# Reordering three places of a two-layer decoder trunk: block copies and writes with the solve's priority, first transposes inside the last product, outputs turned later

## The chip, the cores and the metric

The kernel runs on one NeuronCore of a Trainium2 chip. The metric is the device time of one execution in microseconds. The core has a matrix engine (TensorE, PE in the profile, with its weight loads shown apart as PEld), three engines for elementwise work (VectorE = DVE, ScalarE = ACT, GpSimd = POOL) and an engine that here only issues transfers (SyncE = SP). Each engine works through its own list of instructions in order and waits on semaphores for the others. The order in each list is fixed when the program is built.

## What is computed

The reference takes x (512 tokens by 2048 channels) through two residual layers:

```python
for i in range(DEPTH):                       # DEPTH = 2
    hn = rms_norm(x, norm_w[i])
    if i % 2 == 0:
        out = diff_attention_mixer(hn, ...)  # 8 heads, value width 256
    else:
        out, v_first = rwkv7_mixer(hn, ...)  # 32 heads of 64 channels
    x = x + out
```

The first mixer projects hn to q, k, v and gate (2048 x 8192), takes for each head the difference of two causal softmaxes, multiplies by v, normalises, multiplies by the gate and projects back (2048 x 2048):

```python
a = p[:, :, 0] - lam * p[:, :, 1]
o = rms_norm(einsum('bhqk,bkhd->bqhd', a, v), subln_w) * (1 - lambda_init)
return (o * silu(gate)) @ w_out
```

The second one projects to r, k, v, g and two low-rank inputs, and runs a recurrence on a 64 x 64 state for each head:

```python
sa = einsum('bhvk,bhk->bhv', S, a_t)
S = S * w_t + sa[..., None] * b_t + v_t[..., None] * k_t
y = einsum('bhvk,bhk->bhv', S, r_t)
```

Then it normalises y per head, adds a bonus term, multiplies by silu(g) and projects back.

## The kernel before

**Precision and splitting.** All large products are made in three matmuls: each operand is split into a high part (rounded to the engine's fast 32-bit type) and a low part, and hi x hi, hi x lo and lo x hi are added (`mm3`, from L112). A weight tile comes by DMA into `wraw`; `split_w` (L88 to L104) makes its high part `wh` on ACT (L102) and its low part `wl` on DVE (L103), 128 x 1024 at a time. So each weight tile costs an ACT cast, a DVE subtraction and then its matmuls. The activations' parts are `hH` and `hL`.

**Order.** A scheduling layer sets each engine's order. It places the instructions by their readiness and their priority. `high_priority(offset=...)` raises the priority of what stands inside it; there are three levels, AHEAD 2000, SCAN 3000 and SOLVE 4000 (L39). `issue_after` binds an instruction to stand behind another one. Small work is woven into long runs of projection matmuls: a `Chain` (from L120) is a generator that is resumed by `tick` (L144) after a number of projection matmuls, the number that it yields.

**First layer.** For each of 8 heads, q, k, v and gate are projected while the attention of the head before runs as such a generator, over four blocks of 128 tokens: `scores` makes the softmax difference `a`, `turn` transposes it (into PSUM tag "pb") and splits it into `at` and `al`, `weigh` multiplies with V, normalises and makes `y` (DVE L390), `turn_y` transposes `y` (PE L395) and copies it to `yT` (ACT L396). In one step of the loop `turn`, `turn_y`, eight matmuls of the projection, `weigh` and `scores` follow each other.

**The end of the first layer.** The output projection's second half is made with seven products instead of eight, in Strassen's way (`seven`, from L489). `prod` multiplies one weight sum, `take` (from L520, SCAN; L523) adds a finished PSUM product to the residual rows `xq`, and `done` writes rows and sums their squares (ACT L727). The last product is z with form "22", whose weights lie in tiles named ropeC, ropeS and T (old tables' space). After `seven` the rows are normalised in two halves of the tokens: sums and rsqrt, and for the first half eight scales (L771) with normal priority. Then `half_h` transposes the scaled rows two channel blocks at a time (PE L805 into `xT`, PSUM tag "pa"), and `make_h` makes `hH` on ACT (L857) and `hL` on DVE (L858). These feed the low-rank projection `lora`, and all later projections of the second layer.

**Second layer.** The 32 heads are worked in 16 pairs. For pair j, k, r, v and (three pairs later) g are projected, each 16 weight tiles of 128 columns. The recurrence is made in blocks of 64 tokens. `gram` makes the products within blocks (`gp`, PE L1065), copies them to `G` (ACT L1072, four copies of 128 x 512), sums squares (`ssl`, ACT L1076), and writes the triangular parts of `G` and `ssl` to the DRAM tile `ltd` with six transfers that ACT issues (L1078 for ssl, L1084 for G). `t_solve` (priority SOLVE) loads `ltd` in another layout into `LT` (POOL L1118), and inverts all triangles by 31 steps of two DVE operations each (L1129, L1131), started by L1120 and L1121 and closed by L1132. The result goes out to `td`, and comes back as `TT` by four transfers. `t_combine` transposes a part of it on DVE (`T`, L1155), multiplies (`px`, PE L1161 and L1171) and copies (`X` L1164, `G` L1167, `TT` L1174, all ACT). `scan_pair` then goes through 8 blocks in order, each with three small matmuls that depend on each other: `sm` L1242, a copy to `rhs` on ACT (L1245), `sm` L1253, a copy to `VS` on ACT (L1255), `sm` L1260, an update of `VS` on DVE (L1264 or, for the first block, L1267). `t_combine` and `scan_pair` of one pair are one `Chain`, woven into the projections of the next pair with 6 projection matmuls between the steps and 8 behind the last of a block while pairs 3 to 14 are projected (fewer in the others).

`gram` of pair j calls the next step of the chain of pair j-1 behind its own matmuls. That step is the one that issues `px`. In pair j, px's operand T therefore has to be there by about the time at which the next `gram` is done.

Of the kernel before, what the change touches and what calls it, by code (L numbers as in the profile page):

```python
# [13 lines left out]
F32 = mybir.dt.float32  # L14
# [9 lines left out]
P = 128  # L24
# [3 lines left out]
NT = T // P  # L28
# [10 lines left out]
AHEAD, SCAN, SOLVE = 2000, 3000, 4000  # L39
# [293 lines left out]
def attention(g, h, qkT, qkL, sq, V, VL, G, gap, rows=None):  # L333
# [56 lines left out]
        nc.vector.scalar_tensor_tensor(b.y[:], o[:, :256], ro[:], G[:, t, :], ALU.mult, ALU.mult)  # L390

    def turn_y(t):
        pt = g.ps.tile([P, 512], F32, name="yt", tag="pa", bufs=2)
        for i in range(2):
            nc.tensor.transpose(pt[:, i * P : (i + 1) * P], blocks[t].y[:, i * P : (i + 1) * P], g.ident[:])  # L395
        nc.scalar.copy(yT[:, :, t * P : (t + 1) * P], pt[:, :256].rearrange("p (c q) -> p c q", c=2))  # L396

    for i in range(NT + 3):
        if 0 < i <= NT:
            turn(i - 1)  # L400
        if i > 2:
            turn_y(i - 3)
        if i == NT + 2:
            break
        yield 8
        if 1 < i < NT + 2:
            weigh(i - 2)
        if i < NT:
            scores(i)
        yield gap - 8  # L410
# [75 lines left out]
                          accum_op=ALU.add)  # L486


def seven(g, w, load, rows, sums, c1, c2, acc, Ts, banks, done):  # L489

# [70 lines left out]
    done("22")  # L563
    take("21", X)
    for i in range(N):
        prod(z, i, "22", Ts[i], i == 0, i == last)
    take("21", z)
    done("21")
# [16 lines left out]
def flat(t):  # L585

    n = "abc"[: len(t.shape) - 1]
    n = " ".join(n)
    return t[:].rearrange(f"p {n} -> p ({n})").rearrange("p (k c) -> p k c", k=KG)


def layer0(g, aps):
# [86 lines left out]
    with ExitStack() as cx:  # L679
# [78 lines left out]
        def banks(i):  # L758
            if i < 2:
# [3 lines left out]
        T2 = g.work.tile([P, KG, 512], F32, name="T2", tag="yTh", bufs=1)  # L763
        load = loader(g, aps["da_w_out"][0], ((g.wraw, "wraw", 3), (g.work, "V", 1), (g.wraw, "wraw", 3),
                                              (g.work, "G", 1), (g.wraw, "wraw", 3)))
        seven(g, aps["da_w_out"][0], load, rows, sums, 1024, 1536, acc, [flat(g.C), flat(g.S), T2], banks, done)

        rs = g.work.tile([P, NT], F32, name="rs1", tag="rs1", bufs=1)
        ss = g.work.tile([P, NT], F32, name="ss1", tag="ss1", bufs=1)
        def scale(cb, t):  # L770
            nc.vector.tensor_scalar(xs[cb][:, t, :], xs[cb][:, t, :], rs[:, t : t + 1], None, ALU.mult)  # L771

        for half in (slice(0, 2), slice(2, 4)):
            with tc.high_priority(offset=SOLVE if half.start else 0):
                nc.vector.reduce_sum(ss[:, half], g.ssx[:, half], AX.X)
                nc.vector.tensor_scalar(ss[:, half], ss[:, half], 1.0 / D, EPS, ALU.mult, ALU.add)
                rsqrt(g, rs[:, half], ss[:, half], 2, "r4")
                if half.start == 0:
                    for cb in range(4):
                        for t in range(2):  # L780
                            scale(cb, t)
# [10 lines left out]
                with tc.high_priority(offset=AHEAD):  # L792
                    make_h(g, ps, KT + k)

        def half_h(k, half, m):

            ps = g.ps.tile([P, 512], F32, name="xT", tag="pa", bufs=2)
            for i in range(2):
                xq, c0 = xs[(k + i) // 4], (k + i) % 4 * P
                for t in range(2):  # L800
                    tt, at = 2 * half + t, (2 * i + t) * P
                    if c0 == 0 and half:
                        scale((k + i) // 4, tt)
                    with tc.issue_after(m.ins) if m else ExitStack():
                        nc.tensor.transpose(ps[:, at : at + P], xq[:, tt, c0 : c0 + P], g.ident[:])  # L805
            for i in range(2):
                with tc.high_priority(offset=AHEAD):
                    make_h(g, ps[:, 256 * i : 256 * i + 256], KT + k + i, k + i, half)

        pts = [g.ps.tile([P, 512], F32, name="lora", tag=tag) for tag in ("pb", "pc")]  # L810
        lora = [(aps["rw_w_in"][0], 4 * D, 2 * RK)]

# [5 lines left out]
            return m  # L818


        m, wts = None, []
        turns = [(k, half) for half in range(2) for k in range(0, KT // 2, 2)]
        for i, (k, half) in enumerate(turns):
            if i == 0:
                half_h(k, half, m)
            if i + 1 < len(turns):
                half_h(*turns[i + 1], m)
            else:
                more_h(KT // 2 + 1, m)
            if half == 0 and k % 4 == 0:  # L830
                wts.append(split_w(g, lora, 4, 2 * RK, k))
            for kk in (k, k + 1):
                m = products(kk, wts[kk // 4], slice(256 * half, 256 * half + 256), m)
# [68 lines left out]
C = 64  # L902
# [151 lines left out]
def gram(g, j, p, before):  # L1054
# [12 lines left out]
    if before:  # L1067
        with g.tc.issue_after(m.ins):
            before.step(g)
    for c0, gp in halves:  # L1070
        for h in range(2):
            nc.scalar.copy(p.G[:, c0 : c0 + 4, :, h, :], gp[h][:].rearrange("p (u x t) -> p u x t", u=4, x=2))  # L1072
    ps = g.ps.tile([P, 512], F32, name="pt", tag="pb", bufs=2)
    sum_channels(g, ps[:2, :], g.ones[:, 0 : P : C], p.k2)
    ss = w.tile([2, T], F32, name="ssl", tag="thg", bufs=1)
    nc.scalar.copy(ss[:], ps[:2, :])  # L1076
    for half in range(2):
        nc.scalar.dma_start(  # L1078
            out=g.ltd[j % 2, half, :, :, HALF, :],
            in_=ss[:].rearrange("h (c b t) -> h c b t", c=NC_, b=2)[:, :, half, :])  # L1080
    for half in range(2):
        for h in range(2):
            q0 = h * C + half * HALF
            nc.scalar.dma_start(  # L1084
                out=g.ltd[j % 2, half, h, :, 0:HALF].rearrange("c s t -> s c t"),
                in_=p.G[q0 : q0 + HALF, :, 0, h, half * HALF : (half + 1) * HALF])


def mask_gram(g, p, h):
# [421 lines left out]
```

## Time and profile before

| what | us |
|---|---|
| median of three runs | 2210.98 |
| lowest and highest run | 2207.24, 2213.17 |
| the profiled execution | 2206.95 |
| its span in the profile | 2205.2 |
| PE busy | 2171.5 (98%) |
| DVE busy | 1445.4 (66%) |
| ACT busy | 1041.9 (47%) |
| POOL busy | 293.8 (13%) |

The mean granted clock of TensorE over the execution was 0.993 of full speed. Times in the rows of the profile are microseconds from the start of the span. A row of the timeline gives the start, the duration, the engine, the source line, the operation, the output and inputs with their sizes, how many like it were taken together, and in brackets the idle time before it and what ended it. A row of waits gives the waiting engine and tile, what it waited for, the total, the number of waits and the longest. A row of windows gives a stretch of time, its length, the busy time of PE, PEld, DVE, ACT and POOL with their counts of instructions, the granted clock (1.00 is full speed), the busy share of the DMA engines and their rate. ACTq and POOLq are the DMA issues on these engines. Line numbers are those of the kernel before.

### The profile page before, as it was taken

What the parts mean: (1) busy time and instruction counts of PE and PEld (TensorE: products, weight loads), DVE (VectorE), ACT (ScalarE), POOL (GpSimd) and SP (SyncE); (2) the same over time, 40 slices, a digit from 0 to 9 for tenths busy, and PEclk for the clock granted to TensorE, in tenths of its full rate; (3) what the DMA queues carried; (4) which work ended last, traced back from release to release, by engine and by line L of the source; (5) the groups of instructions that cost most, each with busy time, mean ns of one, the idle gap of its engine ahead of it and who ended that gap; (6) DMA issues with size and microseconds to landing.
All of it is one profiled execution on the core that took longest, in us unless ns stands there. A gap on an engine that the chain in (4) does not pass through costs nothing.

```text
span 2205.2 us, 34098 instructions
## 1 busy us (share of the span) xinstructions
PE 2171.5 (98%) x12260; PEld 1767.9 (80%) x12260; DVE 1445.4 (66%) x3780; ACT 1041.9 (47%) x2118; POOL 293.8 (13%) x637
## 2 busy tenths in 40 slices
PE   9999999999999999999999999999999999999999
PEld 7888888888888888878777787878887788877887
DVE  5664646455654666475667877777778877767644
ACT  5443434334443454345455555555555556545322
POOL 0000000000000000110222222222222222221001
PEclk9999999999999999999999999999999999999999
DMA  6223222222323356653422333333333333446555
GB/s 192 96 79 98 84 96 96 86 96 87 96 77 99 131 171 225 158 117 90 106 57 76 81 87 86 93 97 92 91 87 85 96 91 77 113 123 187 172 167 119
DMA packets 296313, 240.20 MB, mean 109 GB/s; under 512 B 47792, under 2 KB 255680, under 8 KB 296144
## 3 DMA queue, kind: packets, MB, share of 16 engines
q1 hardware_dynamic: 256912, 190.13, 29.3%
q0 software_dynamic: 12384, 29.72, 6.3%
q10 hardware_dynamic: 26848, 18.18, 2.7%
q8 instruction: 96, 1.57, 0.3%
q14 instruction: 73, 0.60, 0.1%
HBM read 217.98 MB, written 19.99 MB: 108 GB/s over the span
## 4 chain that ended last, share of the span: by engine, by line
PE 70%; DVE 19%; issue 4%; DMA 3%; ACT 2%; SPq 0%; POOL 0%; ACTq 0%; DVEq 0%; POOLq 0%
PE pp L114 52%; PE pt L114 5%; DVE wl L103 3%; DVE tmpl L1129 3%; DVE Tm L1131 2%; DMA td<-Tm 2%; DVE VS L1264 1%; PE gp L1065 1%; PE sm L1242 1%; PE lora L114 1%; PE sc L114 1%; PE sm L1260 1%; DMA TT<-td 1%; ACT wh L102 1%; PE sm L1253 1%
## 5 line engine op out<-in xcount | busy, mean ns | idle before, releaser
L103 DVE TENSOR_TENSOR wl<-wraw,wh 128x1024 fp32r<-128x1024 f32 (+2 forms) x319 | 388.9, 1219 | 431.5 <-ACT wh L102 419.0
L102 ACT CAST wh<-wraw 128x1024 fp32r<-128x1024 f32 (+2 forms) x319 | 333.5, 1046 | 513.0 <-PE pp L114 378.3
L114 PE MATMUL pp<-wh,hH 128*128 128x512 f32 x1268 | 499.3, 394 | 0.3 <-DVE gs L326 0.2
L114 PE MATMUL pp<-wh,hL 128*128 128x512 f32 x1268 | 497.7, 393 | 0.1
L114 PE MATMUL pp<-wl,hH 128*128 128x512 f32 x1268 | 497.4, 392 | 0.0
L114 PE MATMUL pp<-hH,wl 128*128 128x512 f32 x1024 | 416.1, 406 | 0.3 <-DVE wl L103 0.3
L114 PE MATMUL pp<-hL,wh 128*128 128x512 f32 x1024 | 415.9, 406 | 0.0
L114 PE MATMUL pp<-hH,wh 128*128 128x512 f32 x1024 | 413.1, 403 | 0.0
L114 PEld LDWEIGHTS pp<-wh,hH 128*128 128x128 f32 x1268 | 238.3, 188 | 48.4 <-PE pp L114 0.6
L114 PEld LDWEIGHTS pp<-wh,hL 128*128 128x128 f32 x1268 | 238.3, 188 | 48.4 <-DVE hL L858 0.5
L114 PEld LDWEIGHTS pp<-wl,hH 128*128 128x128 f32 x1268 | 238.4, 188 | 46.4
L114 PEld LDWEIGHTS pp<-hH,wh 128*128 128x128 f32 x1024 | 194.6, 190 | 36.1 <-issue 0.9
L114 PEld LDWEIGHTS pp<-hL,wh 128*128 128x128 f32 x1024 | 194.6, 190 | 34.9
L114 PEld LDWEIGHTS pp<-hH,wl 128*128 128x128 f32 x1024 | 194.7, 190 | 32.9 <-DVE wl L103 0.7
L1129 DVE SCALAR_TENSOR_TENSOR tmpl<-LT,Tm 128x60 f32<-128x60 f32 (+24 forms) x496 | 135.1, 272 | 10.9
L1248 POOL COPY SA<-VS 64x64 f32<-64x64 f32 x224 | 60.9, 272 | 457.0 <-DVE VS L1264 350.0
L459 POOL DMA_DIRECT2D frow<-yd x12 | 8.9, 746 | 796.4 <-DVE rs_i L63 676.8
L1131 DVE TENSOR_TENSOR Tm<-Tm,tmpl 128x60 f32<-128x60 f32 (+24 forms) x496 | 104.0, 210 | 11.2
L1255 ACT COPY VS<-sm 64x64 f32<-64x64 f32 x256 | 52.9, 207 | 65.8 <-PE sm L1253 61.1
L1245 ACT COPY rhs<-sm 64x64 f32<-64x64 f32 x256 | 52.7, 206 | 53.7 <-PE sm L1242 51.3
L1264 DVE SCALAR_TENSOR_TENSOR VS<-sm,gam,Sg 64x64 f32<-64x64 f32 x192 | 54.1, 282 | 24.7 <-PE sm L1260 20.6
L1251 POOL TENSOR_SCALAR Sg<-SA,gam 128x64 f32<-128x64 f32 x96 | 63.3, 660 | 9.5 <-POOL SA L1248 0.2
(333 smaller groups left out, 3189.6 us busy)
## 6 DMA issues: line engine op xcount, KB each, us to landing
wraw<-in_rw_w_in_dram SPq DMA_DIRECT2D x128, 512.0 KB
wraw<-in_da_w_in_dram SPq DMA_DIRECT2D x254, 256.0 KB
wraw<-in_da_w_out_dram SPq DMA_DIRECT2D x26, 512.0 KB
wraw<-in_rw_w_out_dram SPq DMA_DIRECT2D x26, 512.0 KB
LT<-ltd POOLq DMA_DIRECT2D x64, 132.0 KB, 2.9
yr<-yd SPq DMA_DIRECT2D x28, 256.0 KB
frow<-yd POOLq DMA_DIRECT2D x12, 512.0 KB, 6.9
xq<-in_x_dram SPq DMA_DIRECT2D x16, 256.0 KB
```

What stands on the lines that cost most here:

```text
L102: nc.scalar.copy(hi[:, ks], raw[:, ks])
L103: nc.vector.tensor_sub(lo[:, ks], raw[:, ks], hi[:, ks].bitcast(F32))
L114: m = nc.tensor.matmul(out, a, b, start=s, stop=e, skip_group_check=skip)
L1065: m = nc.tensor.matmul(gp[h][:, i * P : (i + 1) * P], BK[r_, c0 + i, :, :], p.AR[r_, c0 + i, :, :], start=True, stop=True)
L1129: nc.vector.scalar_tensor_tensor(tt, LT[:, i : i + 1, i + 1 :].to_broadcast([P, s, n]), n2[:, i : i + 1], Tm[:, 0:s, i : i + 1].to_broadca ...
L1131: nc.vector.tensor_add(Tm[:, 0:s, i + 1 :], Tm[:, 0:s, i + 1 :], tt)
L1242: nc.tensor.matmul(sm[:, 0:P], both(p.G[:, c, 0]), both(VS[:, c]), start=True, stop=True)
L1245: nc.scalar.copy(rhs[r_, :], sm[r_, h * C : h * C + C])
L1248: nc.gpsimd.tensor_copy(p.SA[r_, c - 1, :], VS[r_, c, h, :])
L1251: nc.gpsimd.tensor_scalar(Sg[:], p.SA[:, c - 1, :], p.gam[:, c : c + 1], None, ALU.mult)
L1255: nc.scalar.copy(VS[r_, c, h, :], sm[r_, P : P + C])
L1264: g.state = nc.vector.scalar_tensor_tensor(VS[r_, c + 1, h, :], s_, p.gam[r_, c : c + 1], Sg[r_, :], ALU.mult, ALU.add)
```

## The change

Three places are reordered. The instructions are the same in number and shape in both kernels.

A. `attention`: `turn_y` stands after the eight matmuls and after `weigh`, and its PSUM tile is of tag "pb", of which there is one buffer and which `turn` uses as well. The last `turn_y` of a head keeps its place.

B. The end of the first layer: `seven` gets a function `begin` that it calls ahead of the last product's last weight tile. `begin` normalises the first half of the tokens, now with priority SCAN, and issues the first two `half_h` transposes (into PSUM tag "pp"). The second half is normalised after `seven`, as before, and the lora loop no longer begins with a transpose of its own.

C. `gram`: the four copies to `G`, the copy to `ssl` and the six writes to `ltd` get the priority SOLVE, and the four writes of G are put ahead of the two writes of ssl.

```diff
     def turn_y(t):
-        pt = g.ps.tile([P, 512], F32, name="yt", tag="pa", bufs=2)
+        pt = g.ps.tile([P, 512], F32, name="yt", tag="pb")
...
     for i in range(NT + 3):
         if 0 < i <= NT:
             turn(i - 1)
+        if i == NT + 2:
+            turn_y(i - 3)
+            break
+        yield 8
+        if i > 1:
+            weigh(i - 2)
         if i > 2:
             turn_y(i - 3)
-        if i == NT + 2:
-            break
-        yield 8
-        if 1 < i < NT + 2:
-            weigh(i - 2)
         if i < NT:
             scores(i)
...
-def seven(g, w, load, rows, sums, c1, c2, acc, Ts, banks, done):
+def seven(g, w, load, rows, sums, c1, c2, acc, Ts, banks, done, begin=None):
...
     for i in range(N):
+        if i == last and begin:
+            begin(g.m)
         prod(z, i, "22", Ts[i], i == 0, i == last)
...
-        seven(g, aps["da_w_out"][0], load, rows, sums, 1024, 1536, acc, [flat(g.C), flat(g.S), T2], banks, done)
...
-        for half in (slice(0, 2), slice(2, 4)):
-            with tc.high_priority(offset=SOLVE if half.start else 0):
+        def normalise(half):
+            with tc.high_priority(offset=SOLVE if half.start else SCAN):
                 nc.vector.reduce_sum(ss[:, half], g.ssx[:, half], AX.X)
...
-        def half_h(k, half, m):
-
-            ps = g.ps.tile([P, 512], F32, name="xT", tag="pa", bufs=2)
+        def half_h(k, half, m, bank=(g.ps, "pa", 2)):
+
+            ps = bank[0].tile([P, 512], F32, name="xT", tag=bank[1], bufs=bank[2])
...
+        def begin(m):
+
+            normalise(slice(0, 2))
+            for k in (0, 2):
+                half_h(k, 0, m, (g.pp, "pp", 4))
+
+        seven(g, aps["da_w_out"][0], load, rows, sums, 1024, 1536, acc, [flat(g.C), flat(g.S), T2], banks, done, begin)
+        normalise(slice(2, 4))
...
-        m, wts = None, []
+        m, wts = g.m, []
...
-            if i == 0:
-                half_h(k, half, m)
-            if i + 1 < len(turns):
+            if 0 < i < len(turns) - 1:
                 half_h(*turns[i + 1], m)
-            else:
+            elif i:
                 more_h(KT // 2 + 1, m)
...
-    for c0, gp in halves:
-        for h in range(2):
-            nc.scalar.copy(p.G[:, c0 : c0 + 4, :, h, :], gp[h][:].rearrange("p (u x t) -> p u x t", u=4, x=2))
+    with g.tc.high_priority(offset=SOLVE):
+        for c0, gp in halves:
+            for h in range(2):
+                nc.scalar.copy(p.G[:, c0 : c0 + 4, :, h, :], gp[h][:].rearrange("p (u x t) -> p u x t", u=4, x=2))
...
-    nc.scalar.copy(ss[:], ps[:2, :])
-    for half in range(2):
-        nc.scalar.dma_start(
-            out=g.ltd[j % 2, half, :, :, HALF, :],
-            in_=ss[:].rearrange("h (c b t) -> h c b t", c=NC_, b=2)[:, :, half, :])
-    for half in range(2):
-        for h in range(2):
-            q0 = h * C + half * HALF
+    with g.tc.high_priority(offset=SOLVE):
+        nc.scalar.copy(ss[:], ps[:2, :])
+    with g.tc.high_priority(offset=SOLVE):
+        for half in range(2):
+            for h in range(2):
+                q0 = h * C + half * HALF
+                nc.scalar.dma_start(
+                    out=g.ltd[j % 2, half, h, :, 0:HALF].rearrange("c s t -> s c t"),
+                    in_=p.G[q0 : q0 + HALF, :, 0, h, half * HALF : (half + 1) * HALF])
+        for half in range(2):
             nc.scalar.dma_start(
-                out=g.ltd[j % 2, half, h, :, 0:HALF].rearrange("c s t -> s c t"),
-                in_=p.G[q0 : q0 + HALF, :, 0, h, half * HALF : (half + 1) * HALF])
+                out=g.ltd[j % 2, half, :, :, HALF, :],
+                in_=ss[:].rearrange("h (c b t) -> h c b t", c=NC_, b=2)[:, :, half, :])
```

## The prediction

> **What bounds the kernel now.** I read the page first (busy shares), then the granted clock in narrow windows, then the groups of waits on PE, and last the timeline at the three places that the change touches.
>
> ```profile
> span 2205.2 us, 34098 instructions
> PE 2171.5 (98%) x12260; PEld 1767.9 (80%) x12260; DVE 1445.4 (66%) x3780; ACT 1041.9 (47%) x2118; POOL 293.8 (13%) x637
> ```
>
> TensorE is busy 98% of the span, so everything the change can win is in the 2% of gaps and in time at a lower clock; any work it moves costs nothing until PE waits for it. The windows show where the clock is lost (columns: window, its length, busy times, then PEclk, DMA share, GB/s):
>
> ```profile
> 1090.00:1095.00 5.00, 2.10 (x24) 1.47 (x22) 1.70 (x3) 0.32 (x1) 2.52 (x9) 1.00 0.80 175
> 1095.00:1100.00 5.00, 5.00 (x31) 3.26 (x30) 0.87 (x2) 1.97 (x4) 2.02 (x3) 0.62 0.76 195
> 1100.00:1105.00 5.00, 5.00 (x42) 4.26 (x41) 0.51 (x1) 1.77 (x3) 0.00 (x0) 0.50 0.00 0
> ...
> 1151.00:1161.00 10.00, 10.00 (x69) 7.44 (x67) 1.97 (x2) 4.11 (x9) 0.00 (x0) 0.50 0.33 86
> 1215.50:1219.00 3.50, 3.50 (x25) 2.56 (x23) 3.16 (x13) 1.08 (x2) 0.00 (x0) 0.52 0.61 166
> ...
> 1949.50:1956.50 7.00, 7.00 (x62) 5.87 (x61) 0.00 (x0) 4.17 (x9) 1.78 (x2) 0.51 0.18 46
> ```
>
> ```profile
> PE px L1161 <- DVE T L1155: 12.5, 13, 3.1
> PE yt L395 <- DVE y L390: 1.5, 8, 0.3
> PEld yt L395 <- DVE y L390: 3.9, 7, 0.6
> PEld sm L1260 <- ACT VS L1255: 16.8, 43, 0.8
> PEld sm L1253 <- ACT rhs L1245: 12.4, 33, 0.6
> ```
>
> ```profile
> 1094.37 0.69 PE L1161 MATMUL px<-T,G 32*32 32x32 f32 x16 [2.90 <-DVE T L1155]
> 1148.83 0.69 PE L1161 MATMUL px<-T,G 32*32 32x32 f32 x16 [1.83 <-DVE T L1155]
> 1213.61 0.69 PE L1161 MATMUL px<-T,G 32*32 32x32 f32 x16 [3.06 <-DVE T L1155]
> 1946.32 0.69 PE L1161 MATMUL px<-T,G 32*32 32x32 f32 x16 [0.46 <-DVE T L1155]
> ```
>
> The waits (total us, times, longest) are those of PE and of its weight load (PEld). The largest one that stops PE is px on T, the end of the solve: 7.8 of its 12.5 us in pairs 0 to 2 (2.90, 1.83, 3.06). Behind each of those the clock stands near 0.5, for about 10, 10 and 3.5 us, and for 7 us after the small one of pair 14 at 1946: some 30 us at half, so 15 us lost, more than the waits themselves. That is the prize of part C.
>
> [...]
>
> **Part A, outputs turned 8 matmuls later (first layer).** The same two transposes and one copy per block, in another bank, behind the 8 matmuls and weigh. Eight 128x512 matmuls (one every 0.23 us in the timeline) are 1.8 us, over the longest wait of 0.6. So up to 1.5 + 3.9 = 5.4 us go; part of the weight loads' 3.9 is already under a running matmul, and the last block of each head keeps its place. I take half, **-2.8 us**, bounds -5.4 and 0. The bank is now shared with turn, whose copies end before weigh starts, so no wait comes in its place; what hides it is those same matmuls.
>
> **Part B, first transposes within the last product.**
>
> ```profile
> 969.31 0.48 DVE L771 TENSOR_SCALAR xq<-xq,rs 128x512 f32<-128x512 f32 x1
> 969.71 1.22 DVE L103 TENSOR_TENSOR wl<-ropeC,wh 128x1024 fp32r<-128x1024 f32 x1
> 970.84 2.47 DVE L523 TENSOR_TENSOR xq<-xq,pp 128x512 f32<-128x512 f32 x4
> ```
>
> ```profile
> 971.15 0.39 PE L114 MATMUL z<-wl,hH 128*128 128x512 f32 x1
> 974.50 0.50 PE L114 MATMUL z<-wl,hH 128*128 128x512 f32 x1 [0.24 <-DVE wl L103]
> 980.00 1.25 PE L805 MATMUL xT<-ident,xq 128*128 128x128 f32 x8 [0.18 <-DVE xq L523]
> 982.34 0.47 PE L114 MATMUL lora<-hH,wh 128*96 128x256 f32 x2 [1.08 <-ACT hH L857]
> 982.97 0.36 PE L114 MATMUL lora<-hL,wh 128*96 128x256 f32 x1 [0.15 <-DVE hL L858]
> 984.22 0.36 PE L114 MATMUL lora<-hL,wh 128*96 128x256 f32 x1 [0.27 <-DVE hL L858]
> ```
>
> The transposes and hH/hL now run under the last product, so the listed waits go: 0.24 + 0.18 + 1.08 + 0.15 + 0.27 = 1.9 us. But the eight scales (L771) and the takes (L523) now carry the scan's priority, and in the changed program's order of DVE all of them stand ahead of the split wl of ropeC, which today runs at 969.71, before the takes. The takes can't start before 970.8 (they wait for the last X matmul), take 2.47, two scales behind them 2 x 0.45, the split 1.22: it ends at about 975.4. The second matmul of z needs it at 971.15. New stall about 4.3 us, at one place; net +2.4. A gap of that length stands beside rows where 1.83 to 3.06 us cost 3.5 to 10 us at half clock, which is 1.7 to 5 us; I take 2.5. **+4.9 us**; bounds -1.9 (the split isn't late) and +7.5. [...]
>
> **Part C, block copies and writes with the solve's priority.** Pair 7, a steady one, today:
>
> ```profile
> 1456.05 2.06 ACT L1072 COPY G<-gp 128x512 f32<-128x512 f32 x4
> 1457.97 0.74 ACT L1174 COPY TT<-px 32x256 f32<-32x256 f32 x2
> 1458.50 0.31 ACTq L1084 DMA_DIRECT2D ltd<-G  x1
> 1458.73 0.58 ACT L1076 COPY ssl<-pt 2x512 f32<-2x512 f32 x1
> 1459.37 1.05 ACT L102 CAST wh<-wraw 128x1024 fp32r<-128x1024 f32 x1
> 1460.32 0.20 ACT L1245 COPY rhs<-sm 64x64 f32<-64x64 f32 x1
> ...
> 1463.96 0.31 ACTq L1084 DMA_DIRECT2D ltd<-G  x1
> ```
>
> ```profile
> 1474.86 1.23 DVE L103 TENSOR_TENSOR wl<-wraw,wh 128x1024 fp32r<-128x1024 f32 x1
> 1476.00 0.59 DVE L1264 SCALAR_TENSOR_TENSOR VS<-sm,gam,Sg 64x64 f32<-64x64 f32 x2
> 1476.63 0.18 DVE L1120 TENSOR_SCALAR LT<-LT 128x32 f32<-128x32 f32 x1
> ```
>
> ```profile
> 1057.74 1.23 DVE L103 TENSOR_TENSOR wl<-wraw,wh 128x1024 fp32r<-128x1024 f32 x1 [4.79 <-ACT wh L102]
> 1058.88 0.17 DVE L1120 TENSOR_SCALAR LT<-LT 128x32 f32<-128x32 f32 x1
> ```
>
> On ACT the changed order is: four G copies, first G write, ssl copy, three G writes, two ssl writes, and only then the TT copies (L1174), rhs and wh. So the last write comes about 3 us earlier than 1463.96, the load of LT with it, and the solve's first operation (L1120) stands ahead of the split and the VS update that precede it today: 1.23 + 0.59 and a part of what is before them, some 2 us. T then comes some 2 us earlier in pairs 3 to 15, against waits under 1 us there: px's remaining 12.5 - 7.8 = 4.7 us go, and with them the half clock at 1949.5 (7.0 us, worth 3.4): **-8.1 us**; bounds -8.1 and 0.
>
> In exchange, what stands behind the copies and writes on ACT is late: TT copies and rhs by about 2 us, and with them the scan's first steps of each pair. In the changed order of PE these steps are put later and then closer together: steps of L1260 that stand only 1 or 2 projection matmuls behind the L1253 they depend on go from 11 to 32, steps of L1253 only 2 or 3 behind L1242 from 15 to 23. A short step of this kind costs today 16.8/43 = 0.39 us and 12.4/33 = 0.38 us (weight-load waits). 21 x 0.39 + 8 x 0.38 = 11.2, and 0.8 for the steps of L1242 that move to 4 or 5 matmuls behind L1260 (21 more): **+12 us**, that is 1.1 in each of the 11 steady pairs. Lower bound half of it (+6: weight loads run beside matmuls); upper bound 11 x 2.6 = 29, if each pair's six squeezed steps, rhs behind a split's cast of 1.05 us among them, all show in full (6 x 0.38 is 2.3, and 0.3 more for the cast).
>
> Pairs 0 to 2: the order puts px earlier too, by 6, 3 and 17 projection matmuls, 1.4, 0.7 and 3.9 us at 0.23. In pair 0 the solve starts right behind the split of 1057.74, which waited 4.79 us for ACT's wh; it starts with no wait of its own, so LT was already there, and an earlier LT gains little: 0.5 us. For pairs 1 and 2 I take 1 and 3.5 us, from what the writes and the splits ahead of the solve free (pair 2's writes are spread widest). Waits: 2.9 + 0.9, 1.8 - 0.3, 3.1 + 0.4: **+1.0 us**, and the 23.5 us at half clock behind them stay. Bounds: +6 if T comes no earlier; -7.8 - 11.7 = -19.5 if all three waits and their clock go. I take the value near the upper end since px and T move together.
>
> SP's queue keeps its order; POOL's queue, which issues the loads of LT, only has them earlier.
>
> **Sum.** -2.8 + 4.9 - 8.1 + 12.0 + 1.0 = **+7.0 us** on the profiled execution (2206.95): 2213.95. That execution lies 4.0 below the median of the three runs shown (2210.98); on the median it gives **2218.0**, 0.3% slower; 0.3% (6.6 us) is about what a measurement of this kernel can tell from no change.
>
> **Rivals.**
> 1. *T really comes early (faster).* The copies and writes end the wait that pairs 0 to 2 show, px no longer stands still, and the half clock behind it goes. T must come 4.3, 2.5 and 7.0 us earlier (today's wait and what px was moved); under that it changes nothing. For it: the clock rows, the largest single loss in the trace. Against it: the row of 1058.88, where LT isn't what the solve waits for. It gives 7.0 - 1.0 - 19.5 = -13.5: 2197.
> 2. *Everything hides (no change that shows).* The squeezed steps cost their lower bound, 6, since their weight loads run beside matmuls, and B's stall costs no clock: -2.8 + 2.4 - 8.1 + 6 + 1 = -1.5: 2209.5. For it: PE is busy 98%. That C doesn't bring T earlier at all, so that the -8.1 stays out, ends here too with the low price (+6.6: 2217.6), at the edge.
> 3. *New stalls lower the clock in the steady pairs (clearly slower).* The row of 1946.32 shows 7 us at half clock after a wait of only 0.46 us and a second small one; the squeezed steps put 1 us and more of waits into a few us in each of 11 pairs. One such window of 3.5 us at half costs 1.7: +19, so 2237; two in each pair give 2256. [...]
>
> **Numbers.** Forecast 0.36, rival 1 0.24, rival 2 0.24, rival 3 0.16. Faster 0.27: rival 1 and a tenth of the forecast. Slower 0.46: rival 3 and most of the forecast. Same 0.27: rival 2 and the rest. Forecast's own range 2211 to 2231 (hop cost 6 to 24). The whole range 2194 to 2243 leaves out the deep end of rival 3 and B's and C's lower bounds taken together.
>
> **What would show it.** A: no wait of yt on y but the last of each head. B: a wait of about 4 us of z on wl at the change of layer, no wait of lora on hH, clock near 0.5 behind it. C: ssl writes behind the G writes, L1120 some 2 us earlier in steady pairs, no px wait from pair 3 on, and PEld waits of L1260 and L1253 about 1.1 us larger per pair; px waits of 2 to 4 us in pairs 0 to 2 with half clock behind. Wrong it would be if px shows no wait in pairs 0 to 2, if the split of ropeC ends in time, or if a steady pair's scan waits add nothing.

## The result: slower by 1.0%

The changed kernel takes 2231.39 us (median of 6 runs, 2224.55 to 2237.05); the kernel before takes 2208.64 us (median of 6, 2202.67 to 2213.17). The ratio is 1.0103 with a 95% interval of 1.0079 to 1.0128, so +22.7 us. The forecast was 2218.0 (+7.0 us), in a range of 2194 to 2243.

The profiled execution of the changed kernel was one of its longer ones: 2237.05 us, span 2235.3 us, 30.1 us more than the profiled execution before. In the changed kernel the lines stand 8 to 11 lower: px is L1172, T L1166, the scan's steps L1253, L1264 and L1271 (before: L1242, L1253 and L1260). In the kernels with C alone and its variants they stand 3 lower (px L1164, T L1158, the scan's steps L1245, L1256 and L1263). The page of the changed kernel:

```profile
span 2235.3 us, 34039 instructions
PE 2193.8 (98%) x12260; PEld 1768.8 (79%) x12260; DVE 1433.8 (64%) x3780; ACT 1040.9 (47%) x2118; POOL 311.8 (14%) x637
```

The waits of PE, and of DVE on the transfer of TT, changed kernel:

```profile
DVE T L1166 <- DMA TT<-td: 40.1, 18, 6.0
PEld sm L1271 <- ACT VS L1266: 30.9, 65, 1.0
...
PEld sm L1264 <- ACT rhs L1256: 16.6, 52, 0.6
...
PE px L1172 <- DVE T L1166: 13.7, 14, 3.7
...
PE sm L1271 <- ACT VS L1266: 4.1, 14, 0.8
PE z L114 <- DVE wl L103: 3.8, 1, 3.8
...
PE yt L395 <- DVE y L390: 0.2, 1, 0.2
```

DVE's wait for that transfer in the kernel before:

```profile
DVE T L1155 <- DMA TT<-td: 20.5, 15, 4.5
```

Five things are to be seen against the rows of before. The waits of yt on y are gone (1.5 to 0.2). A single new wait of 3.8 us stands at z, the place that the prediction named. The scan's short steps wait longer: for VS twice as long (30.9 us in the weight loads and 4.1 on PE, in place of 16.8 and 0.8), for rhs a third longer (16.6 in place of 12.4). px waits for T as it did: 13.7 us in place of 12.5; T was not made earlier for px. And DVE itself stands twice as long for TT, 40.1 us in place of 20.5.

The windows at half clock of the changed kernel (the number behind the busy times of the five engines is PEclk, as before):

```profile
974.70:978.10 3.40, 3.40 (x10) 2.66 (x9) 0.22 (x1) 0.31 (x1) 2.38 (x5) 0.50 0.01 2
1097.60:1111.20 13.60, 13.54 (x86) 10.40 (x87) 4.59 (x6) 2.69 (x6) 3.37 (x4) 0.50 0.55 120
1155.60:1165.80 10.20, 10.20 (x68) 7.67 (x67) 1.28 (x2) 4.83 (x10) 1.98 (x4) 0.50 0.36 93
1213.60:1230.70 17.10, 15.99 (x96) 12.29 (x97) 4.83 (x9) 8.37 (x19) 5.05 (x8) 0.50 0.16 41
1343.40:1346.80 3.40, 3.40 (x44) 3.18 (x43) 0.13 (x1) 2.49 (x6) 0.00 (x0) 0.50 0.16 48
```

That is 47.7 us at half, against 30.7 before (10.2, 10.2, 3.4 and 6.8 us); at half speed 8.5 us more are lost. Where the 30.1 us between the two profiled executions lie can be read from where landmarks stand: the z product begins 1.5 us earlier (969.42 for 970.92); the end of the low-rank products is 2.8 us later (1015.9 for 1013.1), so 4.3 were lost between; `gram` of pair 4 is 9.8 later (1278.5 for 1268.7), 7.0 more, all of it longer half clock; `gram` of pair 14 is 33.1 later (1918.8 for 1885.7), 23.3 more in ten steady pairs; and the end is 30.1 later, 3.0 won back, since there is no half clock at pair 14.

### The profile page after: what moved, and what is told of

The parts are those of the page before. It is cut to its first block, busy times and chain, and to the rows that moved or that the text cites. A ratio compares the mean times of both kernels' runs of the same rounds, so it can differ in the third digit from the quotient of the medians.

```text
span 2235.3 us, 34039 instructions
## 1 busy us (share of the span) xinstructions
PE 2193.8 (98%) x12260; PEld 1768.8 (79%) x12260; DVE 1433.8 (64%) x3780; ACT 1040.9 (47%) x2118; POOL 311.8 (14%) x637
## 4 chain that ended last, share of the span: by engine, by line
PE 71%; DVE 17%; ACT 5%; DMA 3%; issue 3%; POOL 0%; SPq 0%; ACTq 0%; DVEq 0%; POOLq 0%
PE pp L114 53%; PE pt L114 5%; DVE tmpl L1140 3%; DVE wl L103 3%; DVE Tm L1142 2%; DMA td<-Tm 2%; ACT wh L102 2%; PE sc L114 1%; DVE VS L1275 1%; PE gp L1073 1%; PE o L114 1%; PE sm L1271 1%; PE z L114 1%; PE sm L1253 1%; DMA TT<-td 1%
## 5 line engine op out<-in xcount | busy, mean ns | idle before, releaser
L114 PE MATMUL pp<-hH,wl 128*128 128x512 f32 x1024 | 421.8, 412 | 0.1
L1259 POOL COPY SA<-VS 64x64 f32<-64x64 f32 x224 | 69.5, 310 | 454.1 <-DVE VS L1275 387.8
L1278 DVE TENSOR_SCALAR VS<-sm,gam 64x64 f32<-64x64 f32 x32 | 9.1, 283 | 124.7 <-PE sm L1271 124.2
L1256 ACT COPY rhs<-sm 64x64 f32<-64x64 f32 x256 | 52.9, 207 | 46.2 <-PE sm L1253 43.4
L1262 POOL TENSOR_SCALAR Sg<-SA,gam 128x64 f32<-128x64 f32 x96 | 72.4, 754 | 9.4
```

Of the source, the lines that this page charges most:

```text
L114: m = nc.tensor.matmul(out, a, b, start=s, stop=e, skip_group_check=skip)
L1256: nc.scalar.copy(rhs[r_, :], sm[r_, h * C : h * C + C])
L1259: nc.gpsimd.tensor_copy(p.SA[r_, c - 1, :], VS[r_, c, h, :])
L1262: nc.gpsimd.tensor_scalar(Sg[:], p.SA[:, c - 1, :], p.gam[:, c : c + 1], None, ALU.mult)
```

## The experiments

How the table is read: every run has its mean granted clock c. Time x (1 - c) is about what the half clock cost in that run (for the profiled execution before: 2206.95 x 0.007 = 15.4, and half of its 30.7 us at half clock is 15.4). The rest, time x c, is the time outside this loss. Differences of means over the runs, each to the kernel before on the same chip in the same series:

| kernel | ratio of times, 95% interval | difference, us | in half clock | outside it |
|---|---|---|---|---|
| changed kernel (A, B and C) | 1.0103, 1.0079 to 1.0128 | +22.2 | +3.9 | +18.2 |
| A alone | 0.9971, 0.9952 to 0.9989 | -5.8 | -3.1 | -2.7 |
| A alone, again | 0.9963, 0.9947 to 0.9979 | -7.2 | -4.3 | -3.0 |
| B alone | 1.0016, 0.9999 to 1.0033 | +3.1 | +0.7 | +2.4 |
| C alone | 1.0082, 1.0054 to 1.0110 | +17.4 | -1.9 | +19.3 |
| B, normal priority | 1.0009, 0.9991 to 1.0026 | +1.2 | +1.8 | -0.6 |
| C, order of writes alone | 1.0031, 1.0013 to 1.0049 | +6.3 | +3.0 | +3.3 |
| C, writes without priority | 1.0034, 1.0014 to 1.0054 | +7.0 | +3.4 | +3.6 |
| C, ssl and writes with AHEAD | 1.0106, 1.0085 to 1.0127 | +20.5 | +9.9 | +10.6 |
| C, writes issued by SP | 1.0077, 1.0056 to 1.0097 | +16.9 | +11.7 | +5.2 |
| C, writes issued by POOL | 1.0041, 1.0024 to 1.0058 | +9.2 | +12.9 | -3.7 |
| C, scan's copies first | 1.0073, 1.0043 to 1.0102 | +16.4 | +8.1 | +8.4 |
| A and B with normal priority | 0.9986, 0.9963 to 1.0010 | -3.9 | +0.8 | -4.7 |

(For the changed kernel, before is 54 runs of it in three other series, for which the clock is on record.) The clock of a run is given to 0.001, which is 2.2 us; means over 4 to 26 runs are better than that. Over 54 runs of the kernel before, the standard deviation was 1.5 us for the time outside the half clock and 4.3 us for the time lost in it. So differences of 2 us and more in the last column mean something, while in the column before it only the large ones do.

### The three parts alone

A alone is the diff's first piece, B alone the pieces of `seven` and of the end of the first layer, C alone the piece of `gram`.

> Only part A (outputs turned 8 matmuls later). My theory: the waits of yt on y go and z begins 1.5 us earlier, as in the changed kernel; nothing else moves: -1.5 to -2 us. Rival (the freed bank order costs as much in turn or scores): 0 or above.

> Only part B. My theory: z waits about 4 us for the split wl of ropeC, one window of 3.4 us at half clock follows, the lora waits go: the end of lora +4 to +5 us against before, and the whole about +4. Rival (the stall in the changed kernel comes from A's shift or is made good later by more cover in pair 0): 0.

> Only part C. My theory (squeezed scan steps): the way from gram of pair 4 to gram of pair 14 is 640 us instead of 617, and the whole is +20 to +27 us, nearly all that the changed kernel lost. Rival (clock): the steady pairs keep about 62 us each and the loss is in the stretches at half clock of pairs 0 to 3, +7 to +10 us in all.

Outside the half clock the parts add up: -2.7 + 2.4 + 19.3 = 19.0, and all three together cost 18.2. The loss is C's. A alone wins more than the 1.5 to 2 us that I expected: its z begins 2.8 us earlier than in the kernel before (968.08 for 970.92), not 1.5. B alone has the same single wait as the changed kernel, 3.80 us of z on wl, at 975.17. Its low-rank products end at 1018.0, 5.0 us later than before, with 6.8 us at half clock behind the wait. On the whole B costs 3.1 us, and its interval touches no change.

C alone needs 637.6 us from `gram` of pair 4 to that of pair 14 where the kernel before needs 617.0. Only 3.4 us of that stretch are at half clock, so the rival that put the loss into the clock of pairs 0 to 3 falls: C alone has less half clock in all than before (13.7 us in its profile). The waits of C alone:

```profile
PEld sm L1263 <- ACT VS L1258: 30.7, 66, 0.7
PEld sm L1256 <- ACT rhs L1248: 16.9, 52, 0.6
...
PE px L1164 <- DVE T L1158: 11.2, 11, 3.7
```

They are those of the changed kernel. To see where the time goes, I take for each matmul at full clock its lateness: by how much it starts later behind its predecessor than the shortest spacing of two such matmuls in the kernel before. Summed over the ten steady pairs, it rose ahead of `sm` L1260 from 3.1 to 14.4 us (1.1 us for each pair; the expectations further down say 15), ahead of L1253 from 1.1 to 3.7, ahead of L1242 from 5.6 to 7.4, and ahead of the projection's matmuls by 4.8. Together that is 20.5 us; the ten pairs cost 18.9 outside the half clock, as a little came back at `gp` (1.1).

### B with normal priority for the first half

```diff
-            with tc.high_priority(offset=SOLVE if half.start else SCAN):
+            with tc.high_priority(offset=SOLVE if half.start else 0):
```

> Part B, but the first half is normalised and scaled with normal priority as before, so that the split of ropeC can run ahead of the scales. My theory: the 4 us wait of z and the half clock behind it go, some of lora's waits stay away: -2 to 0 us against before. Rival (the split is late because the takes are ahead of it, not the scales): as part B alone, +4.

The wait is gone. DVE of this kernel:

```profile
968.59 1.28 DVE L772 TENSOR_SCALAR xq<-xq,rs 128x512 f32<-128x512 f32 x3
969.78 1.22 DVE L103 TENSOR_TENSOR wl<-ropeC,wh 128x1024 fp32r<-128x1024 f32 x1
970.91 2.48 DVE L523 TENSOR_TENSOR xq<-xq,pp 128x512 f32<-128x512 f32 x4
```

The split of ropeC runs ahead of the takes again. In the changed kernel six scales ran first, and the split was late:

```profile
967.00 2.47 DVE L773 TENSOR_SCALAR xq<-xq,rs 128x512 f32<-128x512 f32 x6
969.38 2.47 DVE L524 TENSOR_TENSOR xq<-xq,pp 128x512 f32<-128x512 f32 x4
971.77 0.87 DVE L773 TENSOR_SCALAR xq<-xq,rs 128x512 f32<-128x512 f32 x2
972.57 1.22 DVE L103 TENSOR_TENSOR wl<-ropeC,wh 128x1024 fp32r<-128x1024 f32 x1
```

So it is the priority of the first half's normalisation, not the moved transposes, that makes B cost anything: 2.9 us lie between the two kernels outside the half clock. The moved transposes themselves win 0.6 us outside the half clock, less than these runs can tell from nothing; the 2 us that I had hoped for at best did not come, and the whole is 1.2 us above before.

### C: which of its pieces

The order of the writes alone, with no priority raised:

```diff
-    with g.tc.high_priority(offset=SOLVE):
+    with g.tc.high_priority(offset=0):
         for c0, gp in halves:
...
-    with g.tc.high_priority(offset=SOLVE):
+    with g.tc.high_priority(offset=0):
         nc.scalar.copy(ss[:], ps[:2, :])
-    with g.tc.high_priority(offset=SOLVE):
+    with g.tc.high_priority(offset=0):
         for half in range(2):
             for h in range(2):
```

> Of part C only the order of the writes (G ahead of ssl), without any priority. My theory: the TT copies and rhs stay ahead of the later writes on ACT, so the scan isn't squeezed: gram 4 to gram 14 617 to 620 us, whole -3 to +3. Rival (the order of the writes itself delays LT, since ssl comes last): +5 or more.

The priority on the copies to G and ssl, not on the writes:

```diff
     with g.tc.high_priority(offset=SOLVE):
         nc.scalar.copy(ss[:], ps[:2, :])
-    with g.tc.high_priority(offset=SOLVE):
+    with g.tc.high_priority(offset=0):
         for half in range(2):
             for h in range(2):
```

> Part C with the priority on the copies to G and ssl alone; the writes in the new order with normal priority. My theory: the block of writes is no longer ahead of TT copies and rhs, only the copies are, which they nearly are in the kernel before too (only ssl passes TT, 0.6 us): gram 4 to 14 about 620 us, whole 0 to +5. Rival (the copies' place, not the writes', squeezes the scan): 635 to 640, +20.

Both are slower than before by 0.3%, half of it outside the half clock (+3.3 and +3.6 us). From `gram` of pair 4 to that of pair 14 they need 623.0 and 619.7 us (633.2 less half of 20.5 at half clock, and 619.7 with none; before 617.0). So the new order of the writes costs some 3 us by itself, which I had expected to be nothing; the priority of the copies to G and ssl adds nothing to it that shows. In both, the lateness ahead of L1260 is 8.4 us (3.1 before) and ahead of L1242 9.8 (5.6 before): the scan's steps move already with the order. What remains of C's 19.3, some 16 us, comes with the priority of the writes.

The priority of ssl and the writes lowered from SOLVE to AHEAD, below the scan's:

```diff
-    with g.tc.high_priority(offset=SOLVE):
+    with g.tc.high_priority(offset=AHEAD):
         nc.scalar.copy(ss[:], ps[:2, :])
-    with g.tc.high_priority(offset=SOLVE):
+    with g.tc.high_priority(offset=AHEAD):
         for half in range(2):
```

> Part C with copies to G at the solve's priority, ssl and the writes at the lowest of the three raised priorities (below the scan's). My theory: the scan's copies stand ahead of the writes again, the writes ahead of casts and other work: gram 4 to 14 617 to 622 us, whole -4 to +4. Rival (any earlier write pulls the solve over the splits and squeezes the scan): as part C alone, +20 and more.

My expectation failed: +20.5 us, as much as C alone, though it is made up in another way, 10.6 outside and 9.9 in the half clock. The scan's steps came back in part: the lateness ahead of L1260 is 9.1 us in the ten pairs instead of 14.4 (before 3.1), ahead of L1253 none. But a wait that is small before (1.8 and 1.3 us, two times each) stands at `gram` now. The waits of this kernel:

```profile
PEld gp L1065 <- DVE AR L1049: 7.6, 11, 1.5
...
PE gp L1065 <- DVE AR L1049: 5.8, 9, 1.1
```

### C with the writes taken off ACT

If the scan is late because ACT is busy with the writes, another engine should issue them.

```diff
-                nc.scalar.dma_start(
+                nc.sync.dma_start(
                     out=g.ltd[j % 2, half, h, :, 0:HALF].rearrange("c s t -> s c t"),
...
-            nc.scalar.dma_start(
+            nc.sync.dma_start(
                 out=g.ltd[j % 2, half, :, :, HALF, :],
```

> Part C, with the six writes issued by SP instead of ACT. My theory (the writes hold up ACT, and the scan's copies TT, rhs and VS are late behind them): the scan keeps its 6 and 8 matmuls, the L1260 waits fall from 15 to 3 to 8 us in the ten steady pairs, and gram 4 to 14 takes 615 to 622 us; whole -5 to +5 us. Rival (the solve that begins earlier takes over the splits and updates and that costs the time, whoever issues): 630 us or more, +10 and more. Where px still waits for T, the early solve wasn't worth anything either way.

The same with `nc.gpsimd.dma_start`:

> Part C, with the six writes issued by POOL instead of ACT. My theory: as with SP for ACT's copies, but POOL also makes SA and Sg for the scan, so that its issues (about 1 us each) hold those up: gram 4 to 14 between 620 and 632 us. Rival (early solve): 630 or more, and the same as with SP.

Half of what I expected came. With SP, the lateness ahead of L1260 fell from 14.4 to 3.7 us, as forecast, and that ahead of L1253 to 1.1, the value of before. So the hold-up on ACT was real. But the ten pairs took 651.1 us, of which 40.6 at half clock: 630.8 with the half clock counted out, not 615 to 622 (POOL: 645.3, 37.5 and 626.5). With SP those are the rival's figures (630 or more, +10 and more); its cause, a price of the early solve whoever issues the writes, fits them. The lateness had moved, to L1242 (15.2 us, before 5.6; PE waits there 8.8 us for DVE's update of VS in the whole kernel, before 3.0) and to `gram`. The timelines of PE and DVE of the kernel with SP, at pair 7's end:

```profile
1522.83 0.69 PE L1164 MATMUL px<-T,G 32*32 32x32 f32 x16 [0.89 <-DVE T L1158]
1524.34 3.62 PE L1065 MATMUL gp<-AR,BK 64*128 64x128 f32 x32 [0.82 <-DVE AR L1049]
```

```profile
1520.76 0.44 DVE L1158 STREAM_TRANSPOSE T<-TT 64x256 f32<-64x256 f32 x1 [5.26 <-DMA TT<-td]
1521.13 1.18 DVE L103 TENSOR_TENSOR wl<-wraw,wh 128x1024 fp32r<-128x1024 f32 x1
1522.33 0.44 DVE L1158 STREAM_TRANSPOSE T<-TT 64x256 f32<-64x256 f32 x1
1522.81 0.75 DVE L898 SCALAR_TENSOR_TENSOR mixr<-pp,prmin_rw_mu_dram,mixr 128x511 f32<-128x511 f32 x1
1523.59 0.69 DVE L1049 TENSOR_TENSOR AR<-mixr,E 128x512 f32<-128x512 f32 x1
```

DVE has the two transposes of T ahead of mixr and AR, the first also ahead of the split; in the kernel before, mixr stands ahead of the first and AR ahead of the second. I take it that the scheduler counts on an early T; the traces show only the order. On the chip T isn't early: DVE stands 5.26 us for the transfer of TT with that work behind it. AR is late for `gram`: PE waits 0.82 us there from pair 4 to pair 14, and 0 to 0.89 us at px just ahead of it. At `gram` of pairs 4 to 13 the clock falls to half each time (the 32 matmuls of `gp` above take 3.62 us instead of 2.06). In this profile the steady pairs alone lose 20.3 us so, and before none; the whole kernel's half clock is 11.7 us dearer than before.

With POOL the time outside the half clock is even lower than before (-3.7), and the whole is slower by 0.4% through the half clock alone. Its profile shows what stands against the steady pairs, with the half clock counted out: these cost 9.5 us (626.5 for 617.0), but the way from `gram` of pair 0 to that of pair 4 is 4.0 us shorter (212.7 for 216.7), and what follows `gram` of pair 14 is 5.8 us shorter (310.3 for 316.1). The issue of a write of G on POOL took 0.60 us in it (at 1516.81 us), where about 1 us was expected.

### C with the scan's copies first

```diff
-            nc.scalar.copy(rhs[r_, :], sm[r_, h * C : h * C + C])
+            with g.tc.high_priority(offset=SOLVE):
+                nc.scalar.copy(rhs[r_, :], sm[r_, h * C : h * C + C])
```

and so for the copies to TT (L1174) and VS (L1255).

> Part C as in the change, but the scan's own copies on ACT (TT, rhs, VS) have the solve's priority too, so that they stand ahead of the writes again, which ACT still issues. My theory (of C's 18.6 us outside the half clock most is the scan held up on ACT): the waits of L1260 in the ten steady pairs fall from 15 to under 9 us, those of L1253 to 1; time outside the half clock +1 to +8 us against before. What it costs in half clock I leave open: with T ahead of other work on DVE, as with SP and POOL, +9 to +15 us; without, 0. Rival (the early solve costs the time whoever waits on ACT): +14 us or more outside the half clock.

L1260's lateness is 9.1 us and L1253's none, about as expected; outside the half clock the kernel costs 8.4 us instead of C's 19.3, just above the 8 that I had allowed, and far under the rival's 14. So a good half of C's cost outside the half clock goes when the scan's copies stand ahead of the writes on ACT. What stays in the ten pairs is lateness ahead of L1260 (6.0 us more than before), L1242 (4.3) and `gp` (1.9); the first two are little more than what the order of the writes alone gave (5.3 and 4.2). In the half clock it costs 8.1 us. Here too T's first transpose stands ahead of mixr and AR on DVE, and the steady pairs have two stretches of 10.2 us, behind waits at px and `gp` of 0.83 and 0.67 us (at `gram` of pair 9) and of 1.23 and 0.67 us (pair 12). In the steady pairs this kernel is nearly the one with ssl and writes at AHEAD: the same lateness ahead of L1260 and L1253, and 627.2 and 627.0 us without the half clock.

### What can be kept

> Parts A and B, B with normal priority for the first half, without C. If the parts add: A's -3.4 us and B's -1.3 us outside the half clock, -4.7 in all, and a half clock as in the kernel before (within 3 us): 0.3% faster. Rival (the gain of A was in the half clock alone, by luck): within 0.1% of before.

> Part A alone once more, with more runs. The first time it was 0.29% faster, half of it outside the half clock (-3.4 us) and half in it (-3.4). If the time at half clock is chance, this time the part outside comes again (-2.5 to -4.5 us) and the half clock is within 2.5 us of before: 0.1 to 0.25% faster. If part A really takes half clock away (it ends 3 us earlier, so that all later gaps fall at other times), the half clock is again 3 us or more lower: 0.25 to 0.35% faster.

Outside the half clock A and the mended B together win 4.7 us. The table's single figures add up to less, 3.3 or 3.6 us (the two expectations above go by an earlier reckoning, -3.4 and -1.3); means of ten runs with a scatter of 1.5 us don't tell the two apart. In the half clock they gave +0.8, so that the whole, 0.9986, isn't clear of no change. A alone is faster than the kernel before in both series, 0.9971 and 0.9963; of this, 2.7 and 3.0 us lie outside the half clock, where the removed waits are. The half clock was lower both times too (-3.1 and -4.3). But the kernel with A and the mended B has the same waits removed and no lower half clock, and no profile shows why A alone should have one. Whether that part of A's gain is chance stays open.

## Why the prediction was right, and where it was not

**Direction and size.** Slower was forecast, by 7.0 us; it is 22.7 us. The measured time is in the whole range and just past the upper end of the forecast's own range (2211 to 2231). Two terms of the sum were wrong by 8 to 9 us each, both in C and both on the same side, so that the time is in the range by the range's width and not by the sum.

**A, -2.8 us:** -2.7 and -3.0 outside the half clock. The lower half clock wasn't forecast.

**B, +4.9 us:** the wait of z is 3.80 us (4.3 forecast), at the place and for the reason named (of the two priorities named, only that of the scales was new; the takes had the scan's before too), followed by 3.4 us (in B alone 6.8 us) at half clock. The listed waits, 1.9 us that were to go, went only in part: in the kernel without the z wait 1.2 us of such waits remain, and it wins 0.6 us. As a whole B cost 3.1.

**C, squeezed steps, +12 us:** the mechanism was right, and the price too low. The ten pairs cost 20.6 us in C alone, 2.1 each and not 1.1 (18.9 and 1.9 with the half clock counted out); that is between the forecast and its upper bound of 2.6. Mis-sized was the step that priced only the 29 steps that came closer together, at the mean wait of before, 0.38 us. The waits of the weight loads did grow by the 1.1 us per pair that the prediction gave as a sign (18.3 us more in 16 pairs); but they are not all that is late. ACT in pair 7 of the changed kernel shows what else is late:

```profile
1474.62 0.58 ACT L1086 COPY ssl<-pt 2x512 f32<-2x512 f32 x1
1474.68 1.31 ACTq L1091 DMA_DIRECT2D ltd<-G  x3
1476.09 1.27 ACTq L1095 DMA_DIRECT2D ltd<-ssl  x2
1477.69 0.74 ACT L1185 COPY TT<-px 32x256 f32<-32x256 f32 x2 [2.49 <-DMA ltd<-G]
1478.43 0.43 ACT L1256 COPY rhs<-sm 64x64 f32<-64x64 f32 x2
```

The five issues behind the ssl copy take 2.6 us together, and ACT's computing part stands 2.49 us for them (2.2 to 3.2 us in each of pairs 4 to 13). TT, rhs and the casts to wh behind them are late, and the projection's own matmuls start later too (+4.8 us in the ten pairs, which the sum did not have).

**C, T earlier, -8.1 us:** this step failed, and the term comes to nothing. "The solve's first operation stands ahead of the split and the VS update" came true; "T then comes some 2 us earlier" didn't. The same rows of DVE as in the prediction, changed kernel, pair 7:

```profile
1490.76 0.59 DVE L1275 SCALAR_TENSOR_TENSOR VS<-sm,gam,Sg 64x64 f32<-64x64 f32 x2
1491.39 0.18 DVE L1131 TENSOR_SCALAR LT<-LT 128x32 f32<-128x32 f32 x1
...
1492.16 1.22 DVE L103 TENSOR_TENSOR wl<-wraw,wh 128x1024 fp32r<-128x1024 f32 x1
...
1525.16 0.42 DVE L1143 TENSOR_TENSOR Tm<-Tm,LT 128x256 f32<-128x256 f32 x1
...
1533.86 0.44 DVE L1166 STREAM_TRANSPOSE T<-TT 64x256 f32<-64x256 f32 x1 [2.82 <-DMA TT<-td]
```

The end of the solve and T in pair 7 of the kernel before:

```profile
1507.99 0.42 DVE L1132 TENSOR_TENSOR Tm<-Tm,LT 128x256 f32<-128x256 f32 x1
...
1514.46 0.44 DVE L1155 STREAM_TRANSPOSE T<-TT 64x256 f32<-64x256 f32 x1 [1.09 <-DMA TT<-td]
```

Counted from `gram`'s start (1470.9; before 1454.5), the solve begins at 20.4 us (before 22.1), but ends at 54.6 (53.9). The other steady pairs agree: on the mean of pairs 4 to 13 the last write is issued 3.3 us earlier and the last load of LT 4.0, and the solve starts 1.6 earlier (20.6 for 22.2) but ends 0.7 later (54.7 for 54.0). With SP and POOL, which start it earlier still (19.9 and 19.5), it ends at 54.3 and 53.6. The split and the VS update that stood ahead of it before now run inside it. DVE has about the same work up to the end of the solve, whatever its order, and there is hardly idle time in the solve that an earlier start could use: 1.7 of 31.8 us before, 2.5 of 34.2 now. Behind it, the trip to `td` and back took longer as well: T begins at 62.9 (59.9 before; 61.7 for 59.5 on the mean of the ten pairs). The traces name a likely reason. From the issue of the write to `td` to that of the loads of TT it is 4.7 us (3.4 before), and the last load of a weight tile is now issued 0.6 us ahead of that write, before 2.8. Over the nine profiles with C's variants the two go together: 3.2 to 3.7 us where the weight load lies 2.6 or 2.8 us ahead, 4.5 to 5.1 where it lies 0.6 or 0.8 ahead. No run moved the weight load alone, so this isn't shown as the cause. So px waits as before, and the steady pairs' waits that the sum took away stayed.

**Pairs 0 to 2, +1.0 us, and the half clock there stays:** right in the main. px's waits are 3.74, 1.71 and 2.12 us (2.90, 1.83 and 3.06 before; 3.8, 1.5 and 3.5 forecast), so that of pair 2 fell where a rise was forecast, and from `gram` of pair 0 to that of pair 4, with half of the time at half clock taken out, the kernel needs 215.2 us (216.8 before). The half clock in that stretch was 41 us in one profile and 10.2 in the one of C alone, with nearly the same waits.

**The rivals.** "T really comes early" did not happen in the changed kernel. A part of its prize came with the writes off ACT: with SP px waits 1.77 us in pair 0 and not at all in pairs 1 and 2, with POOL 1.98, 0.97 and 0.56, and from `gram` of pair 0 to that of pair 4 the two have 10.6 and 6.8 us at half clock (23.9 before; but A alone had 6.8 too, with px's waits as before). "New stalls lower the clock in the steady pairs" did not happen in the changed kernel, whose ten steady pairs had 3.4 us at half clock. It did happen with SP in all of pairs 4 to 13 and with POOL in eight of them, around waits of 0.82 us at `gp` and 0 to 0.89 us at px ahead of it. The traces show no total of waits from which the clock falls: 0.46 and 0.67 us were followed by half clock at `gram` of pair 15 of the kernel before, 0.97 and 0.38 at that of its pair 11 were not.

## What to carry to other kernels

Before an operation is moved ahead on an engine that works almost without gaps, ask what it passes: the passed work doesn't vanish, and if the chain needs the same engine till its end, the end hardly moves (here from 0.3 us earlier to 0.7 us later for starts 1.6 to 2.7 us earlier). A transfer's issue is an instruction too: at a high priority, the issues of the writes held up the scan's copies behind them for 2.2 to 3.2 us in each steady pair. And an instruction placed ahead of the time at which its operand comes makes what stands behind it wait too: with SP, at pair 7's end, DVE stood 5.26 us for the transfer of TT ahead of T's first transpose, mixr and AR came behind it, and PE waited 0.82 us for AR.

When the clock moves between runs, split each run's time into time x (1 - clock) and the rest: here the parts of the change added up in the rest, and a gain there was lost again in the clock with the writes on POOL.

## What the hardware showed that I had not expected

The same wait is followed by very different times at half clock. The kernel with A alone was profiled twice, on two chips. px of pair 0 waits 2.83 us in the one and 3.04 us in the other:

```profile
1091.38 0.93 PE L1162 MATMUL px<-T,G 32*32 32x32 f32 x16 [2.83 <-DVE T L1156]
```

```profile
1092.12 1.06 PE L1162 MATMUL px<-T,G 32*32 32x32 f32 x16 [3.04 <-DVE T L1156]
```

Behind the first the half clock lasts 3.4 us (1091.6 to 1095.0), and the clock is full in the window from 1095.6; behind the second it stays at half for 13.6 us. First the one, then the other, as windows:

```profile
1095.60:1099.00 3.40, 3.40 (x47) 2.65 (x44) 0.00 (x0) 2.22 (x6) 0.00 (x0) 1.00 0.09 22
```

```profile
1092.20:1105.80 13.60, 13.60 (x89) 10.56 (x89) 3.24 (x4) 4.86 (x10) 2.57 (x3) 0.50 0.26 75
```

In the profiles of the kernel before and of the changed kernel, all stretches at half clock (but one that begins 1 us before the changed kernel's end) last 3.4 us or 2 to 5 times that (10.2, 10.2, 3.4 and 6.8 us before; 3.4, 13.6, 10.2, 17.1 and 3.4 us in the changed kernel). They also begin a whole number of such steps apart: in the kernel before at 1096.2, 1150.8, 1215.6 and 1949.5 us, which is 16, 19 and 215 steps of 3.413 us (853.3 us in 250 steps), in the changed kernel at 974.7, 1097.6, 1155.6, 1213.6 and 1343.4 us, which is 36, 17, 17 and 38. The clocks of 54 runs of the kernel before lie between 0.989 and 0.998, so the half clock costs one and the same kernel between 4 and 24 us. The prediction, with its fixed lengths, had not allowed for that. What sets the number of steps behind a wait was not shown.

Nor did a wait's length, or the sum of two, decide in these runs whether the clock fell. With SP, gaps of 0.82 us at `gp` with 0 to 0.89 us at px ahead of them were followed by half clock in ten pairs. With POOL, pair 5 has the very waits of the rows of SP above, 0.89 and 0.82 us, and stays at full clock, with its 32 matmuls of `gp` in 2.06 us:

```profile
1317.45 0.69 PE L1164 MATMUL px<-T,G 32*32 32x32 f32 x16 [0.89 <-DVE T L1158]
1318.96 2.06 PE L1065 MATMUL gp<-AR,BK 64*128 64x128 f32 x32 [0.82 <-DVE AR L1049]
```
